# A hybrid encoder layer on one core: the tokens normalised and transposed in two halves, with the V projection between them

## The chip, the core and the metric

The kernel runs on one core of a Trainium2 chip. The metric is the device time of one execution in microseconds, as the median of several executions. The core has four compute engines, which follow their own instruction streams and wait for each other by semaphores: TensorE (PE in the rows; PEld is its loading of weights), VectorE (DVE), ScalarE (ACT) and GpSimd (POOL). SyncE (SP) issues nearly all DMA transfers. Each engine works through its own stream in order, so an instruction that waits holds up everything behind it on its engine.

## The reference

One layer for 512 tokens of width 1024, all float32. The part that the change touches first:

```python
h = rmsnorm(x, pre_mix_norm[l])
proj = h @ w_in[l]
z, xbc, dt_raw, q, k, v, gates = split_cols(proj, IN_SPLITS)
y_ssd = ssd_branch(z, xbc, dt_raw, ...)       # a bidirectional state-space scan, 32 heads
y_attn = window_attention(q, k, v, ...) @ w_attn_out[l]
mixed = (g_ssd * y_ssd + g_attn * y_attn) @ w_o[l]
x = x + rmsnorm(mixed, post_mix_norm[l])
h = rmsnorm(x, pre_mlp_norm[l])
f = jnp.square(jax.nn.relu(h @ w_mlp_in[l])) @ w_mlp_out[l]
x = x + rmsnorm(f, post_mlp_norm[l])
```

## The kernel before

Every product of float32 operands is made of three matmuls on rounded parts: each operand is split into a high part `hi` and a remainder `lo`, and `hi*hi`, `hi*lo` and `lo*hi` are summed in PSUM (`mm3`). So each chunk of weights (128 x 1024 values, 512 KB) is loaded to a raw tile `wr`, ScalarE casts it to `wh`, and GpSimd or VectorE subtracts to get `wl`, in four pieces. Three buffers each hold raw chunks, `wh` and `wl`.

The work is a list of quanta. A quantum is mostly one projection block of 128 output columns for all 512 tokens: 8 steps of k by 3 matmuls, 24 matmuls of 512 columns into one bank of PSUM. `cm` makes such blocks. `tm` makes the V projection with the tokens on the output's partitions: two quanta of two token tiles each (`pair(0)` and `pair(1)`), each 48 matmuls of 256 columns, tile by tile, over two chunks of weights. `dt` (64 columns) is 16 matmuls of 512 columns. The list begins with the two K blocks, then V, dt, and two query blocks.

Before the first quantum, `start` loads the eight tiles of x (four token tiles `t`, two halves `j` of the width, 256 KB each), the identity `ident` for transposes and the gain vector `g`. ScalarE and VectorE square a tile each and sum it, GpSimd makes the reciprocal root `rst`, VectorE scales the tile, and TensorE transposes it in eight 128 x 128 pieces into eight banks of PSUM, one for each k. When all four token tiles are there, ScalarE and VectorE make `h`, hi and lo, from each bank (512 columns at once). Meanwhile `WARM` matmuls on a zero tile keep TensorE busy.

The eight banks of PSUM form two rings: three are called `pp` (blocks of projections), five `ps` (everything else). A tile of a ring waits until the tile that held its bank before has been read for the last time.

The order of the instructions on every engine is not the order of the code. The class `Planner` takes all recorded instructions, with a cost for each, and simulates the five streams; the order that it finds is then forced. So a change of its numbers, or of the code, can move instructions anywhere.

In the MLP, `up_halves` makes the first three blocks for the first 256 tokens before the second 256 have been normalised, and finishes them afterwards; `up_done` then takes relu squared, in place in the bank, and `combine` reads two such banks until its line 1358. At the very end, `down_done` adds the last bank to `acc`, ScalarE squares it for the norm, VectorE multiplies it by the gain `g4`, GpSimd takes the reciprocal root, VectorE scales and adds, and SyncE stores.

Some small constants are broadcast to all partitions by DMA at the start: `dtb` (two rows of 64, for `dt_bias` and `a_log`), `sink` (16) and `dsk` (32, the skip gains, copied by VectorE into `dcol`).

Of the kernel before, what the change touches and what calls it, by code (L numbers as in the profile page):

```python
# [10 lines left out]
F32 = mybir.dt.float32  # L11
F32R = mybir.dt.float32r
AF = mybir.ActivationFunctionType
# [6 lines left out]
NT = 4  # L20
# [10 lines left out]
WARM = 10  # L31
# [44 lines left out]
class Planner:  # L76
# [120 lines left out]
    def duration(self, n):  # L197
# [16 lines left out]
        columns = sum(1 for a in ins if size(a) == 1 and w > 1)  # L214
        if e == "ACT":
            c = (170 if psum else 205) + 0.82 * w + (175 if len(outs) > 1 else 0)
            return c + (85 if columns else 0) * (w < 512 or columns > 1), False
# [10 lines left out]
    def deadlines(self):  # L228

        at, t = {}, 0.0  # L230
        for n, e in enumerate(self.eng):
            if e == "PE":
                at[n] = t
                t += self.cost[n][0]
        late = [0.0] * len(self.ins)
        for n in reversed(range(len(self.ins))):
            e, c = self.eng[n], self.cost[n][0]
            if e == "PE":
                late[n] = at[n]
                continue  # L240
            c += 4000 if e == "SP" else 0
            late[n] = min([late[s] - self.AFTER[self.eng[s]] for s in self.post[n]] + [t + 5000.0]) - c
        return late

    def plan(self, wait=0.3):
# [12 lines left out]
        for _ in self.ins:  # L258
# [20 lines left out]
            if e == "SP":  # L279
                aps = self.operands(self.ins[n].outs)  # L280
                size = 4 * math.prod(d[1] for d in aps[0].ap)
                queue = max(queue, t + 900) + size / 230
# [5 lines left out]
            else:  # L288
# [4 lines left out]
                free[e] = end - self.OVERLAP[e]  # L293
            for s in self.post[n]:
# [22 lines left out]
class Trunk:  # L317
# [196 lines left out]
    def tm(self, c, done):  # L514
# [5 lines left out]
        def pair(t2):  # L520
            ps = self.bank("pp")
# [16 lines left out]
    def start(self):  # L538
        nc = self.nc
        get, put = self.slots.get, self.slots.put  # L540
        self.ident = self.const("ident", [128, 128])
        g = get("g", (128, 128))
        xt = []
        for t in range(NT):
            xt.append([get("x") for _ in range(2)])
            for j in range(2):
                nc.sync.dma_start(xt[t][j], self.d_x[0, t * 128:(t + 1) * 128, j * 512:(j + 1) * 512])
            if t == 0:
                nc.sync.dma_start(self.ident, self.d_cst[:, :128])
                nc.sync.dma_start(g[:8], self.d_pre_mix_norm[0].rearrange("(k p) -> k p", p=128))  # L550
        self.prefetch(2, 0)
# [4 lines left out]
        nc.sync.dma_start(cst, self.d_cst[:, 128:])  # L556
        self.mhalf = self.const("mhalf", [128, 1])
        nc.vector.memset(self.mhalf, -0.5)


        ssq = self.const("ssq0", [128, 8])
        rst = self.const("rst0", [128, 4])
        gT = self.const("gT", [128, 8])
        zero = get("zero", (128, 128))
        nc.vector.memset(zero, 0.0)
        pg = self.bank("ps")
        for _ in range(WARM):
            self.mm(pg[:, :128], zero, zero, True, True)
        put(zero)
        pg = self.bank("ps")  # L570
        self.tr(pg[:, :8], g[:8, :])
        nc.vector.tensor_copy(gT, pg[:, :8])
        put(g)
        ps = [self.bank(tag) for tag in ["pp"] * 3 + ["ps"] * 5]
        for t in range(NT):
            junk = [get("junk") for _ in range(2)]
            nc.scalar.activation(junk[0], xt[t][0], AF.Square, scale=D ** -0.5, accum_out=ssq[:, 2 * t:2 * t + 1])
            nc.vector.tensor_tensor_reduce(junk[1], xt[t][1], xt[t][1], 1.0 / D, EPS, ALU.mult, ALU.add, ssq[:, 2 * t + 1:2 * t + 2])
            put(*junk)
            r = rst[:, t:t + 1]  # L580
            nc.gpsimd.tensor_tensor(r, ssq[:, 2 * t:2 * t + 1], ssq[:, 2 * t + 1:2 * t + 2], op=ALU.add)
            nc.gpsimd.tensor_tensor(r, r, self.mhalf, op=ALU.pow)
            for j in range(2):
                nc.vector.tensor_scalar(xt[t][j], xt[t][j], r, None, op0=ALU.mult)
            for k in range(8):
                self.tr(ps[k][:, t * 128:(t + 1) * 128], xt[t][k // 4][:, (k % 4) * 128:(k % 4 + 1) * 128])
            put(*xt[t])
        self.h = []
        self.prefetch(2, 1)
        for k in range(8):  # L590
            hi, lo = get("h", dtype=F32R), get("h", dtype=F32R)
            self.split_by(hi, lo, ps[k], gT[:, k:k + 1])
            self.h.append((hi, lo))
        self.show("hT", self.h[3][0].bitcast(F32))
# [161 lines left out]
    def kv_quanta(self):  # L756
# [22 lines left out]
        return [self.cm(self.d_w_in, C_K + 128 * i, hh, k_done, ("pppp", "vvpp")[i]) for i in range(2)] + self.tm(C_V, v_done)  # L779
# [594 lines left out]
    def up_halves(self, n):  # L1374
# [148 lines left out]
    def down_done(self, j, t, ps, col):  # L1523
# [17 lines left out]
        nc.vector.tensor_tensor(a, a, self.g4[j][:, col], op=ALU.mult)  # L1541
        if j == 1 and col.stop == 512:
            r = rs[:, n % 2:n % 2 + 1]
            nc.gpsimd.tensor_tensor(r, r, self.mhalf, op=ALU.pow)  # L1544
            for i in range(2):
                x1 = self.x1[t][i]
                for c in [slice(0, 512)] if t < 3 or i == 0 else [slice(0, 256), slice(256, 512)]:
                    nc.vector.scalar_tensor_tensor(x1[:, c], self.acc[t, i][:, c], r, x1[:, c], op0=ALU.mult, op1=ALU.add)  # L1548
# [3 lines left out]
    def build(self):  # L1552
# [3 lines left out]
        self.pair, self.held = [], {}  # L1556
# [4 lines left out]
        self.add(*self.kv_quanta())  # L1561
        self.add(self.dt_quantum())
# [70 lines left out]
```

## Time and profile before

| | |
|---|---|
| median of 3 runs | 1102.45 us (1101.1 to 1104.1) |
| the profiled execution | 1101.8 us, of which its span is 1099.7 us |
| TensorE busy | 1084.1 us, 99% of the span |
| VectorE, ScalarE, GpSimd busy | 711.8, 622.2, 771.5 us |
| DMA | 128 MB, 116 GB/s over the span |

The span is what the profile covers, from the first instruction to the last; 2.1 us of the profiled execution lie outside it. A busy TensorE can still be one that runs at half its clock, so the clock column of the stretches is read beside it.

### The profile page before, as it was taken

To read this page: it belongs to the slowest core of one execution; us is meant where nothing else is said; L and a number is where in the kernel's file an instruction comes from. 1 tells how busy PE (TensorE), PEld (TensorE's weight loads), DVE (VectorE), ACT (ScalarE), POOL (GpSimd) and SP (SyncE) were. 2 spreads that over 40 slices of the span, in tenths; PEclk is the share of its full clock that TensorE was granted. 3 is DMA by queue.
4 is the path that set the end of the run, shared out by engine and by line. 5 is a ranking of instruction groups with operands and counts; after the bars stand their busy time and mean duration, and the time that the engine had idled before them with its cause. 6 is when DMAs were issued, how large, how long until landed. Compare 5 with 4: busy or idle time off the path is not lost.

```text
span 1099.7 us, 16603 instructions
## 1 busy us (share of the span) xinstructions
PE 1084.1 (99%) x5651; PEld 910.7 (83%) x5651; DVE 711.8 (65%) x1229; ACT 622.2 (57%) x1325; POOL 771.5 (70%) x946
## 2 busy tenths in 40 slices
PE   8999999999999999999999999999999999999997
PEld 6988888888888888888888788889788888888886
DVE  6287787687687687788877852425555566564135
ACT  5356776687667767676778532324555444444331
POOL 4436666557668798899989966511679898898842
PEclk8999999999999999999999999999999999999999
DMA  6434433534444536364655563603312522523232
GB/s 191 138 94 118 125 97 100 149 89 115 108 119 140 134 102 174 87 157 122 155 133 149 151 176 114 191 21 115 96 39 77 173 58 81 169 58 98 65 107 76
DMA packets 207584, 128.09 MB, mean 116 GB/s; under 512 B 10851, under 2 KB 192595, under 8 KB 207500
## 3 DMA queue, kind: packets, MB, share of 16 engines
q1 hardware_dynamic: 207500, 127.04, 40.9%
q8 instruction: 44, 0.72, 0.3%
q14 instruction: 40, 0.33, 0.1%
HBM read 124.59 MB, written 2.42 MB: 116 GB/s over the span
## 4 chain that ended last, share of the span: by engine, by line
PE 61%; POOL 1%; DVE 1%; ACT 1%; issue 1%; POOLq 0%; DVEq 0%
PE pp L375 45%; PE ps L375 16%; PE ps L379 1%; POOL wl L454 0%; POOL w L1104 0%; DVE x L1548 0%; POOL frs L1544 0%; POOL w L1103 0%; ACT junk L1534 0%; DVE acc L1532 0%; ACT m L1068 0%; DVE m L1069 0%; POOL ssq L1111 0%; ACT wh L450 0%; DVE yT L1142 0%
## 5 line engine op out<-in xcount | busy, mean ns | idle before, releaser
L454 POOL TENSOR_TENSOR wl<-wr,wh 128x256 fp32r<-128x256 f32 (+1 forms) x513 | 439.6, 885 | 185.6 <-ACT wh L450 180.1
L375 PE MATMUL pp<-h,wh 128*128 128x512 f32 (+1 forms) x1760 | 534.8, 386 | 2.6 <-DVE ft L1356 2.1
L375 PEld LDWEIGHTS pp<-h,wh 128*128 128x128 f32 x1760 | 324.5, 188 | 66.6 <-ACT wh L450 2.3
L375 PE MATMUL pp<-h,wl 128*128 128x512 f32 (+1 forms) x872 | 336.3, 386 | 0.0
L450 ACT CAST wh<-wr 128x1024 fp32r<-128x1024 f32 (+1 forms) x141 | 146.8, 1043 | 172.5 <-PE pp L375 123.7
L375 PEld LDWEIGHTS pp<-h,wl 128*128 128x128 f32 x872 | 163.9, 188 | 32.0
L1452 POOL TENSOR_TENSOR wl<-wd,wh 128x256 fp32r<-128x256 f32 x144 | 117.0, 848 | 13.4 <-ACT wh L1449 11.9
L375 PE MATMUL ps<-wh,fl 128*128 128x512 f32 (+1 forms) x192 | 73.0, 380 | 0.0
L375 PE MATMUL ps<-wh,fh 128*128 128x512 f32 (+1 forms) x192 | 73.0, 380 | 0.0
L375 PE MATMUL ps<-wl,fh 128*128 128x512 f32 (+1 forms) x192 | 73.0, 380 | 0.0
L1067 ACT ACTIVATE n<-cb,tables 128x128 f32<-128x128 f32 x128 | 49.1, 391 | 19.7 <-DVE cb L1058 19.5
L1449 ACT CAST wh<-wd 128x512 fp32r<-128x512 f32 x72 | 41.5, 618 | 31.3 <-PE ps L375 19.8
L899 DVE SCALAR_TENSOR_TENSOR u<-pp,cv,u 128x510 f32<-128x510 f32 (+1 forms) x64 | 47.7, 745 | 5.7 <-ACT u L895 4.3
L1068 ACT ACTIVATE m<-cb,tables 128x128 f32<-128x128 f32 x128 | 48.9, 388 | 3.0 <-DVE cb L1058 3.0
L375 PE MATMUL pp<-yh,wl 128*128 128x512 f32 x128 | 49.9, 390 | 0.3 <-POOL wl L454 0.3
L375 PE MATMUL pp<-yl,wh 128*128 128x512 f32 x128 | 49.8, 389 | 0.0
L375 PE MATMUL pp<-yh,wh 128*128 128x512 f32 x128 | 49.7, 389 | 0.0
L1063 ACT ACTIVATE rf<-rf,tables 128x128 f32<-128x128 f32 x128 | 42.3, 393 | 12.1 <-DMA rf<-csT 12.0
L831 ACT ACTIVATE P<-P,mx 128x384 f32<-128x384 f32 (+1 forms) x64 | 35.2, 553 | 20.5 <-DVE mx L828 20.2
L1061 POOL TENSOR_TENSOR rb<-rb,tables 128x512 f32<-128x512 f32 x32 | 35.7, 1119 | 12.8 <-DMA rb<-csT 5.1
L1103 POOL TENSOR_TENSOR w<-w,E 128x256 f32<-128x256 f32 x48 | 38.4, 812 | 6.3 <-DVE w L1099 4.8
L1320 DVE SCALAR_TENSOR_TENSOR pp<-pp,r 128x256 f32<-128x256 f32 (+1 forms) x24 | 13.5, 563 | 44.7 <-ACT r L1316 44.5
(244 smaller groups left out, 2053.4 us busy)
## 6 DMA issues: line engine op xcount, KB each, us to landing
wr<-in_w_in SPq DMA_DIRECT2D x76, 512.0 KB, 3.9
wr<-in_w_mlp_in SPq DMA_DIRECT2D x32, 512.0 KB, 4.0
wd<-in_w_mlp_out SPq DMA_DIRECT2D x48, 256.0 KB, 4.7
rf<-csT SPq DMA_DIRECT2D x32, 256.0 KB, 4.2
rb<-csT SPq DMA_DIRECT2D x32, 256.0 KB, 5.0
wr<-in_w_ssd_out SPq DMA_DIRECT2D x14, 512.0 KB, 4.6
E<-csE SPq DMA_DIRECT2D x96, 64.0 KB, 3.9
x<-in_x SPq DMA_DIRECT2D x16, 256.0 KB, 3.8
```

The source lines that it names most:

```text
L375: self.nc.tensor.matmul(out, lhsT, rhs, start=start, stop=stop, skip_group_check=more)
L450: self.nc.scalar.copy(hi[:, :m], raw)
L454: engines[e].tensor_tensor(lo[:, c], raw[:, c], hi[:, c].bitcast(F32), op=ALU.subtract)
L831: nc.scalar.activation(p[:, :w], p[:, :w], AF.Exp, bias=mx[:, n:n + 1], accum_out=sm[:, n:n + 1])
L899: nc.vector.scalar_tensor_tensor(u[:, a:e], ps[:, a + d:e + d], self.wtap(t, b), u[:, a:e], op0=ALU.mult, op1=ALU.add)
L1061: nc.gpsimd.tensor_tensor(v4(rb), v4(rb), cs[:, 1].unsqueeze(2).to_broadcast([128, 4, 128]), op=ALU.subtract)
L1063: nc.scalar.activation(v4(rf)[:, h], v4(rf)[:, h], AF.Identity, bias=ncs[:, 0, h:h + 1])
L1067: nc.scalar.activation(v4(n)[:, h], cb[:, 0], AF.Copy, scale=dt[:, 0, h:h + 1])
L1068: nc.scalar.activation(v4(m)[:, h], cb[:, 1], AF.Copy, scale=dt[:, 1, h:h + 1])
L1103: nc.gpsimd.tensor_tensor(wc, wc, E[:, d], op=ALU.add)
L1449: nc.scalar.copy(hi[:, cols], src)
L1452: (nc.vector if q == 512 else nc.gpsimd).tensor_tensor(lo[:, c], src[:, e * q:(e + 1) * q], hi[:, c].bitcast(F32), op=ALU.subtract)
```

## The change

Four edits of the program, and the planner's numbers for DMAs.

1. `start` is split. `start_half(0)` loads, normalises and transposes token tiles 0 and 1 before the first quantum, into four banks (two k to a bank) instead of eight; `start_half(1)` does tiles 2 and 3 and is recorded at quantum 1. `h` is made in pieces of 256 columns. V's two quanta now come first, then dt, then K. Tile j = 0 is scaled by ScalarE, no longer by VectorE. V's first pair uses a bank of the ring `ps`.
2. The identity and the gain vector are issued on ScalarE's queue ahead of its table load; `WARM` goes from 10 to 20, and 8 more matmuls on a scaled tile follow the transposes of token tile 0. The table of constants `cst` is recorded after the first half.
3. `up_halves` takes its third bank from `ps`.
4. In the tail the product with the gain goes to a new tile `ag` instead of back into `acc`.

```diff
-WARM = 10
+WARM = 20
...
+        if e == "ACT" and "DMA" in kind:
+            return 400, False
...
-            c += 4000 if e == "SP" else 0
+            c += 4000 if "DMA" in type(self.ins[n]).__name__ else 0
...
-                queue = max(queue, t + 900) + size / 230
+                queue = max(queue, t + 900) + size / 300
...
+                end += 2500 if "DMA" in type(self.ins[n]).__name__ else 0
...
-            ps = self.bank("pp")
+            ps = self.bank("pp" if t2 else "ps")
...
         self.ident = self.const("ident", [128, 128])
+        nc.scalar.dma_start(self.ident, self.d_cst[:, :128])
         g = get("g", (128, 128))
+        nc.scalar.dma_start(g[:8], self.d_pre_mix_norm[0].rearrange("(k p) -> k p", p=128))
...
+        self.h = [(get("h", dtype=F32R), get("h", dtype=F32R)) for _ in range(8)]
+        self.start_half(0)
+        self.prefetch(2, 1)
+        self.at(1, lambda: self.start_half(1))
+        self.at(1, self.later_constants)
+
+    def start_half(self, t2):
+
+        nc = self.nc
+        get, put = self.slots.get, self.slots.put
+        xt = {}
+        for t in (2 * t2, 2 * t2 + 1):
+            xt[t] = [get("x") for _ in range(2)]
             for j in range(2):
                 nc.sync.dma_start(xt[t][j], self.d_x[0, t * 128:(t + 1) * 128, j * 512:(j + 1) * 512])
+        ps = [self.bank(tag) for tag in (["ps"] * 4 if t2 else ["pp"] * 3 + ["ps"])]
+        for t in xt:
+            junk = [get("junk") for _ in range(2)]
+            ssq, r = self.ssq0[:, 2 * t:2 * t + 2], self.rst0[:, t:t + 1]
+            nc.scalar.activation(junk[0], xt[t][0], AF.Square, scale=D ** -0.5, accum_out=ssq[:, 0:1])
+            nc.vector.tensor_tensor_reduce(junk[1], xt[t][1], xt[t][1], 1.0 / D, EPS, ALU.mult, ALU.add, ssq[:, 1:2])
+            put(*junk)
+            nc.gpsimd.tensor_tensor(r, ssq[:, 0:1], ssq[:, 1:2], op=ALU.add)
+            nc.gpsimd.tensor_tensor(r, r, self.mhalf, op=ALU.pow)
+            nc.scalar.activation(xt[t][0], xt[t][0], AF.Copy, scale=r)
+            nc.vector.tensor_scalar(xt[t][1], xt[t][1], r, None, op0=ALU.mult)
+            for k in range(8):
+                self.tr(ps[k % 4][:, k // 4 * 256 + t % 2 * 128:k // 4 * 256 + t % 2 * 128 + 128],
+                        xt[t][k // 4][:, (k % 4) * 128:(k % 4 + 1) * 128])
             if t == 0:
+                for _ in range(8):
+                    self.mm(self.dummy[:, :128], xt[t][1][:, :128], xt[t][1][:, :128], True, True)
+            put(*xt[t])
+        tok = slice(t2 * 256, t2 * 256 + 256)
+        for k in range(8):
+            hi, lo = self.h[k]
+            self.split_by(hi[:, tok], lo[:, tok], ps[k % 4][:, k // 4 * 256:k // 4 * 256 + 256], self.gT[:, k:k + 1])
...
-        return [self.cm(self.d_w_in, C_K + 128 * i, hh, k_done, ("pppp", "vvpp")[i]) for i in range(2)] + self.tm(C_V, v_done)
+        return self.tm(C_V, v_done) + [self.cm(self.d_w_in, C_K + 128 * i, hh, k_done) for i in range(2)]
...
-                banks.append(self.bank("pp"))
+                banks.append(self.bank("pp" if m < 2 else "ps"))
...
-        nc.vector.tensor_tensor(a, a, self.g4[j][:, col], op=ALU.mult)
+        if col.start == 0:
+            self.ag[t, j] = self.slots.get("ag")
+        nc.vector.tensor_tensor(self.ag[t, j][:, col], a, self.g4[j][:, col], op=ALU.mult)
...
-        self.add(*self.kv_quanta())
-        self.add(self.dt_quantum())
+        kv = self.kv_quanta()
+        self.add(*kv[:2], self.dt_quantum(), *kv[2:])
```

Three places show how instructions move. The first is SyncE's stream from the dt bias to the skip gains, with the DMA semaphore that each issue waits for (a DMA waits for the last DMA that used its semaphore). Before:

```order
L634 DMA v_49_467<-in_pre_mlp_norm 8x128 [waits DMAHW4_49]
L556 DMA cst<-in_cst 128x448 [waits DMAHW5_49]
L360 DMA dtb<-in_dt_bias 128x64 [waits DMAHW6_49]
L360 DMA sink<-in_attn_sink 128x16 [waits DMAHW7_49]
L360 DMA dtb<-in_a_log 128x64 [waits DMAHW0_49]
L360 DMA dsk_550<-in_d_skip 128x32 [waits DMAHW1_49]
```

Now, where `wr_199` is the weights of dt (256 KB) and the last one on semaphore 6 ahead of `dtb`:

```order
L433 DMA wr_199<-in_w_in 128x8x64 [waits DMAHW6_49]
L641 DMA v_45_482<-in_conv_w 112x128 [waits DMAHW7_49]
L642 DMA v_46_483<-in_conv_w 48x128 [waits DMAHW0_49]
L643 DMA v_46_483<-in_conv_b 32x128 [waits DMAHW1_49]
L644 DMA v_46_483<-in_b_gate 16x128 [waits DMAHW2_49]
L645 DMA v_46_483<-in_ssd_norm 16x128 [waits DMAHW3_49]
L646 DMA v_46_483<-in_pre_mlp_norm 8x128 [waits DMAHW4_49]
L606 DMA cst<-in_cst 128x448 [waits DMAHW5_49]
L363 DMA dtb<-in_dt_bias 128x64 [waits DMAHW6_49]
L363 DMA dtb<-in_a_log 128x64 [waits DMAHW7_49]
L363 DMA sink<-in_attn_sink 128x16 [waits DMAHW0_49]
L363 DMA dsk_622<-in_d_skip 128x32 [waits DMAHW1_49]
```

`a_log` has moved ahead of `sink`; `dsk` is still the last of the four. Before, the transfer on semaphore 6 ahead of `dtb` was a V chunk of 512 KB (`wr_227`, of line 430); now it is dt's chunk of 256 KB.

The second place is VectorE's stream at the start. Before, the copies of `dsk` into `dcol` stand behind all of h:

```order
L401 SCALAR_TENSOR_TENSOR h_220<-ps_122,gT,h_219 128x512
L401 SCALAR_TENSOR_TENSOR h_224<-ps_123,gT,h_223 128x512
L454 TENSOR_TENSOR wl_232<-wr_91,wh_231 128x256 x2
L612 COPY dcol<-dsk_550 64x16 x2
L767 TENSOR_TENSOR KL_271<-pp_245,KH_270 64x512
```

Now (x_277 to x_282 are token tiles 2 and 3, ps_285 the first of their banks):

```order
L404 SCALAR_TENSOR_TENSOR h_119<-ps_131,gT,h_118 128x256
L583 ISA junk_290,ssq_75<-x_278 128x512
L583 ISA ssq_75 128x1
L583 ISA junk_306,ssq_75<-x_282 128x512
L583 ISA ssq_75 128x1
L671 COPY rows_271<-ps_269 16x512
L624 COPY dcol<-dsk_622 64x16 x2
L588 TENSOR_SCALAR x_278<-x_278,rst_76 128x512
L588 TENSOR_SCALAR x_282<-x_282,rst_76 128x512
L404 SCALAR_TENSOR_TENSOR h_105<-ps_285,gT,h_104 128x256
```

The copies now stand between the squares of the second half's tiles and their scaling. On ScalarE likewise the exponential of `a_log` (line 729, before 717) now stands ahead of the scaling of the second half's other two tiles.

The third place is TensorE where the first three blocks of the MLP end and the fourth begins. Before:

```order
L375 MATMUL pp_8332<-h_901_8174,wh_7946 128x256
L375 MATMUL pp_8332<-h_902_8175,wh_7946 128x256
L375 MATMUL pp_8332<-h_901_8174,wl_7947 128x256
L375 MATMUL pp_8526<-h_887_8160,wh_8423 128x512
L375 MATMUL pp_8526<-h_888_8161,wh_8423 128x512
```

Now:

```order
L378 MATMUL ps_8366<-h_901_8208,wh_7980 128x256
L378 MATMUL ps_8366<-h_902_8209,wh_7980 128x256
L378 MATMUL ps_8366<-h_901_8208,wl_7981 128x256
L378 MATMUL pp_8560<-h_887_8194,wh_8457 128x512
L378 MATMUL pp_8560<-h_888_8195,wh_8457 128x512
```

The order is the same; the third block's bank is now of the other ring, so that the fourth block (pp_8560) takes the third `pp` bank, last used in the mix, instead of the first block's.

## Rows read from the trace of the kernel before

**Rows 1.** Waits of TensorE, whole span: us in total, times, longest.

```profile
PE pp L379 <- DMA ident<-in_cst: 3.4, 1, 3.4
PE pp L375 <- DVE ft L1356: 2.1, 1, 2.1
PE ps L375 <- ACT pT L848: 0.8, 1, 0.8
```

**Rows 2.** Timeline, start: us, us long, engine, line, tiles, count, idle before.

```profile
1.03 4.24 PE L375 MATMUL ps<-zero 128*128 128x128 f32 x20 [1.03 <-DVE zero L565]
8.61 0.49 DVE L584 TENSOR_SCALAR x<-x,rst 128x512 f32<-128x512 f32 x1 [1.00 <-POOL rst L582]
8.64 0.45 PE L379 MATMUL pp<-ident,x 128*128 128x128 f32 x1 [3.37 <-DMA ident<-in_cst]
10.02 0.16 DVE L572 COPY gT<-ps 128x8 f32<-128x8 f32 x1
11.75 1.05 ACT L450 CAST wh<-wr 128x1024 fp32r<-128x1024 f32 x1 [1.80 <-DMA wr<-in_w_in]
16.33 0.73 PE L375 MATMUL pp<-h,wh 128*128 128x512 f32 x2 [0.52 <-DVE h L401]
```

**Rows 3.** Stretches: us, PE, PEld, DVE, ACT, POOL busy, clock, DMA share, GB/s.

```profile
8.00:15.00 7.00, 6.36 (x29) 5.84 (x29) 4.77 (x11) 2.42 (x6) 3.87 (x8) 0.51 1.09 307
16.33:43.60 27.27, 27.27 (x163) 23.64 (x164) 13.51 (x20) 15.34 (x26) 12.08 (x17) 1.00 0.44 122
```

**Rows 4.** Timeline of SyncE's queue, 15 to 18 us.

```profile
15.79 0.35 SPq L360 DMA_DIRECT2D dtb<-in_dt_bias  x1
16.66 0.44 SPq L360 DMA_DIRECT2D dtb<-in_a_log  x1
17.15 0.43 SPq L360 DMA_DIRECT2D dsk<-in_d_skip  x1
```

**Rows 5.** Timeline: readers of the last constants, and GpSimd beside them.

```profile
20.55 7.36 POOL L454 TENSOR_TENSOR wl<-wr,wh 128x256 fp32r<-128x256 f32 x10 [4.17 <-ACT wh L450]
21.97 0.26 ACT L717 ACTIVATE dtb<-dtb 128x64 f32<-128x64 f32 x1 [0.55 <-DMA dtb<-in_a_log]
22.36 1.38 DVE L612 COPY dcol<-dsk 64x16 f32<-64x16 f32 x2
```

**Rows 6.** Timeline, TensorE in the first query projection.

```profile
44.31 0.39 PE L375 MATMUL pp<-h,wl 128*128 128x512 f32 x1
```

**Rows 7.** GpSimd's splits up to 45 us: busy us, mean ns, idle before.

```profile
L454 POOL TENSOR_TENSOR wl<-wr,wh 128x256 fp32r<-128x256 f32 x21 | 15.4, 770 | 13.6 <-ACT wh L450 13.6
```

**Rows 8.** Timeline, a flip of half the tokens before the MLP.

```profile
742.68 1.91 PE L379 MATMUL ps<-ident,h 128*128 128x128 f32 x16
743.46 2.29 ACT L400 ACTIVATE h<-ps,cv 128x256 fp32r<-128x256 f32 x6
746.09 2.04 DVE L401 SCALAR_TENSOR_TENSOR h<-ps,cv,h 128x256 fp32r<-128x256 f32 x5
```

**Rows 9.** Chain that ended last, 764 to 810 us: start, us, what.

```profile
765.87 6.36 PE pp L375 x52
776.24 0.34 DVE ft L1356
776.72 1.40 PE pp L375 x5
804.21 5.44 PE ps L375 x24
```

**Rows 10.** Timeline there, TensorE and GpSimd.

```profile
774.33 0.28 PE L375 MATMUL pp<-h,wl 128*128 128x256 f32 x1
771.46 10.09 POOL L454 TENSOR_TENSOR wl<-wr,wh 128x256 fp32r<-128x256 f32 x12 [9.48 <-ACT wh L450]
```

**Rows 11.** GpSimd in the tail, and line 370: ns min/median/max.

```profile
1094.26 0.66 POOL L1544 TENSOR_TENSOR frs<-frs,mhalf 128x1 f32<-128x1 f32 x1 [3.00 <-DVE frs L1539]
L370 POOL TENSOR_TENSOR rs<-rs,mhalf x8: 537/543/553, 722.4 to 761.4; 128x1 f32<-128x1 f32 x8
```

More of the change, by code (lines that the diff above doesn't have):

```diff
@@ L541, in start @@
         self.ident = self.const("ident", [128, 128])
+        nc.scalar.dma_start(self.ident, self.d_cst[:, :128])
         g = get("g", (128, 128))
-        xt = []
-        for t in range(NT):
-            xt.append([get("x") for _ in range(2)])
+        nc.scalar.dma_start(g[:8], self.d_pre_mix_norm[0].rearrange("(k p) -> k p", p=128))
+        self.mhalf = self.const("mhalf", [128, 1])
+        nc.vector.memset(self.mhalf, -0.5)
+        self.ssq0 = self.const("ssq0", [128, 8])
+        self.rst0 = self.const("rst0", [128, 4])
@@ new lines, in start @@
+        self.gT = self.const("gT", [128, 8])
+        zero = get("zero", (128, 128))
+        nc.vector.memset(zero, 0.0)
+        self.dummy = self.bank("ps")
+        for _ in range(WARM):
+            self.mm(self.dummy[:, :128], zero, zero, True, True)
+        put(zero)
+        pg = self.bank("ps")
+        self.tr(pg[:, :8], g[:8, :])
+        nc.vector.tensor_copy(self.gT, pg[:, :8])
+        put(g)
+        self.h = [(get("h", dtype=F32R), get("h", dtype=F32R)) for _ in range(8)]
+        self.start_half(0)
@@ L546, in start @@
+        self.prefetch(2, 1)
[7 more added lines that the diff above has]
+            xt[t] = [get("x") for _ in range(2)]
             for j in range(2):
                 nc.sync.dma_start(xt[t][j], self.d_x[0, t * 128:(t + 1) * 128, j * 512:(j + 1) * 512])
-            if t == 0:
-                nc.sync.dma_start(self.ident, self.d_cst[:, :128])
-                nc.sync.dma_start(g[:8], self.d_pre_mix_norm[0].rearrange("(k p) -> k p", p=128))
@@ L551, in start @@
-        self.prefetch(2, 0)
+        ps = [self.bank(tag) for tag in (["ps"] * 4 if t2 else ["pp"] * 3 + ["ps"])]
[12 more added lines that the diff above has]
+                        xt[t][k // 4][:, (k % 4) * 128:(k % 4 + 1) * 128])
+            if t == 0:
+                for _ in range(8):
+                    self.mm(self.dummy[:, :128], xt[t][1][:, :128], xt[t][1][:, :128], True, True)
+            put(*xt[t])
@@ L552, in start, with later_constants @@
+        tok = slice(t2 * 256, t2 * 256 + 256)
+        for k in range(8):
+            hi, lo = self.h[k]
+            self.split_by(hi[:, tok], lo[:, tok], ps[k % 4][:, k // 4 * 256:k // 4 * 256 + 256], self.gT[:, k:k + 1])
+    def later_constants(self):
         cst = self.const("cst", [128, 448])
@@ L555, in start @@
         self.UL = cst[:, :256].rearrange("p (d s) -> p d s", d=2)
[L556 to L594, printed above, removed]
+        self.nc.sync.dma_start(cst, self.d_cst[:, 128:])
     def transpose_split(self, src, name, tag="ps"):
@@ L1547, in down_done @@
                 for c in [slice(0, 512)] if t < 3 or i == 0 else [slice(0, 256), slice(256, 512)]:
-                    nc.vector.scalar_tensor_tensor(x1[:, c], self.acc[t, i][:, c], r, x1[:, c], op0=ALU.mult, op1=ALU.add)
+                    nc.vector.scalar_tensor_tensor(x1[:, c], self.ag[t, i][:, c], r, x1[:, c], op0=ALU.mult, op1=ALU.add)
                     nc.sync.dma_start(self.out[0, t * 128:(t + 1) * 128, i * 512 + c.start:i * 512 + c.stop], x1[:, c])
@@ L1555, in build @@
         self.h2t, self.h2, self.f, self.acc = [], [], {}, {}
-        self.pair, self.held = [], {}
+        self.pair, self.held, self.ag = [], {}, {}
         n = lambda: len(self.quanta)
```

## Prediction

> **What bounds the kernel now.** I read TensorE's waits first, because the page has TensorE busy for 99% of the span. In the whole span three waits stand out: 3.4 us for the identity, 2.1 us for a bank that VectorE has to read (line 1356), 0.8 us for the scores' softmax [rows 1]. So no edit can bring more than it does in one of three places: ahead of TensorE's first gapless stretch, at that bank, or behind its last matmul. Second I read the start's timeline: ten matmuls on the zero tile, 4.24 us long (20 records, two to a float32 matmul, so 0.42 us each), an idle wait of 3.37 us, transposes from 8.64, the first projection at 16.33 [rows 2]. Third the stretches: from 16.33 to 43.60 TensorE is busy 27.27 of 27.27 us at full clock, while from 8 to 15 us the clock is 0.51 and DMA moves 307 GB/s [rows 3]. So the measure for the start is when the two K blocks, V and dt are all done, that is, when the first query block begins. Its third matmul begins at 44.31; two matmuls of 0.2267 us earlier (24 in 5.44 us [rows 9]) is 43.86 [rows 6].
>
> **The start, part by part.** *Weights.* Four x tiles instead of eight lie ahead of the weights, 1 MB less. At 307 GB/s that is 3.4 us, so the first cast goes from 11.75 [rows 2] to about 8.35 and ends 1.05 later, at 9.4. GpSimd then makes eight pieces of `wl` at 0.77 us [rows 7], 6.2 us, to 15.6. The first token tile needs both V chunks, all eight pieces. It ends some three matmuls behind the last of them; the second tile is 24 matmuls of 256 columns at 0.122 us (52 in 6.36 us [rows 9]), 2.9 us. V's first quantum is done at about 18.9.
>
> *The second half.* It can't follow at once. In VectorE's new order the two copies of `dsk` stand ahead of the scaling of tiles 2 and 3, and on ScalarE the exponential of `a_log` does. So the scaling waits for the last of the small broadcasts. Before, `dtb`, `a_log` and `dsk` were issued at 15.79, 16.66 and 17.15 [rows 4]; the reader of `a_log` began at 21.97, waiting for its DMA, and the copies of `dsk` at 22.36 [rows 5]: `dsk` landed between, and I take 22.15. The transfer whose semaphore `dtb` waits for is now 256 KB instead of 512 KB, 0.85 us less at 307 GB/s, so `dsk` lands at about 21.3 (bounds 21.3 and 22.15, if the issue is not earlier). The copies took 1.38 us for two, 0.69 each, beside GpSimd's splits from 20.55 to 27.9 [rows 5]; the nearest copy with GpSimd not splitting, of 8 columns, took 0.16 [rows 2]. Now GpSimd has no chunk to split then. I take 0.16 each, with 0.69 as the other bound: 21.65. Two scalings of 0.49 [rows 2] end at 22.65, transposes of the last tile close the first bank 0.2 later, ScalarE's first piece of h takes 0.38 and VectorE's eight take 0.41 each [rows 8]: 0.2 + 0.38 + 3.3 gives 26.55. The last bank's three matmuls end about 0.35 later, at 26.9; V's other matmuls have gone in between.
>
> The rule that decides between the two prices of the copy is in the Trainium skill, "SBUF — State Buffer", section "Who interferes with whom": VectorE and GpSimd share one pair of ports, a copy can take it, and who comes second is blocked for a whole instruction of the other. By it the 0.69 holds a wait for GpSimd, and without splits the copy is short; by the row alone the same copies cost 0.69 again, and the sum would be 1.06 us more.
>
> *Behind it* 24 matmuls of V at 0.122 (2.9), 14 of dt at 0.2267 (3.2; two of the 16 are earlier) and 48 of K (10.9) follow without a gap, 17.0 us in all: the first query block begins at 43.9, where it was 43.86. **The start gives nothing**: TensorE begins its projections some four microseconds earlier, and idles from about 18.9 to 22.1 instead.
>
> *Free edits.* Ten more warming matmuls are 4.2 us at the row's rate and end between 7.2 and 9.5 (the bounds: all faster once the clock rises, or none). Their cover is TensorE's 3.37 us wait for the identity [rows 2], which the earlier issue on ScalarE takes away. If they end at 9.5 with the eight dummies behind, the first half is about 1.4 us later, V's first quantum later by up to 2.1 with it (21.0), still ahead of 22.1. So they cost nothing while the second half is what is late. The two issues on ScalarE (0.35 to 0.44 each by SyncE's [rows 4]) lie ahead of the first x tile.
>
> **The MLP.** The third half block's last matmul begins at 774.33 [rows 10], 0.122 us long, and the next block begins at 776.72, behind the first block's relu squared and its combination on VectorE, which starts at 776.24 [rows 9]. The weights are not the cause, since GpSimd splits from 771.46 on [rows 10]. In the new order the fourth block takes the third `pp` bank, last used in the mix and long free. The removed wait is 776.72 - 774.33 - 0.12 = **2.27 us**. The next stall would be the fifth block's bank, the first block's: it comes free where the fourth began before, at about 776.7, and is wanted only after the fourth block's work, which began at 774.45 and lasts 5.4 us (24 x 0.2267), at 779.9. So nothing is late next. The bounds are 0, if another wait stands there, and 2.27.
>
> **The tail.** In place, VectorE's product with the gain had to wait until ScalarE had squared the tile, and so ran beside the last reciprocal root; into a new tile it can run ahead. That root took 0.66 us where eight others took 0.543 in the middle [rows 11]. I take 0.12 us off, bounds 0 and 0.12.
>
> **Everything else** (h in pieces of 256 columns, the planner's numbers) I set to 0. TensorE's order behind K is the same, and its remaining wait there is 0.8 us [rows 1]: that is the most to gain, and as much again may be lost.
>
> **Sum:** 0 - 2.27 - 0.12 = about -2.4 us. Against its own time, 1101.8 becomes 1099.4; the median of the runs shown is 0.65 above that profiled execution, so 1102.45 becomes **1100.1**.
>
> **Rivals.**
> *The second half isn't held up.* If the constants land earlier or the order leaves slack, GpSimd's sums and roots for tiles 2 and 3 come behind its splits (15.6) with four small instructions, at about 17.1; scaling ends at 18.1, TensorE is free at 18.9, the first bank closes at 20.5, and the same 0.38 + 3.3 + 0.35 gives 24.5 instead of 26.9. The start then gains 2.3 us: 1097.8. Against it: the issue rows and the order of VectorE, which put `dsk` near 21.3.
> *The clock falls in the new idle time (the slower side).* The stretch from 8 to 15 us ran at 0.51, the lower level of 1.2 GHz, behind an idle wait of 3.37 us [rows 2, 3]. The new wait from 18.9 to 22.1 is 3.2 us long and comes behind a stretch in which TensorE follows GpSimd's pieces and is busy about half. If the clock is low when the second half begins, the 16 transposes, V and dt's first matmuls take twice as long: some 6.8 us of work at half rate, so that the chain ends near 29.5 instead of 26.9, 2.6 us later: 1102.9. It is slower than before from 2.4 us of such loss on; if the low clock lasts through twice as much work, it is 1106.5. For it: those rows. Against it: the ten warming matmuls went at the low rate already, so that no row shows a fall. The Trainium skill, "TensorE: Matmul & The Clock Gate", Part 1, says that the slow clock is the default and activity releases it; by that rule this rival's 1102.9 is what the pause makes.
> *The constants land no earlier and the copies stay long.* 0.85 + 1.06 = 1.9 us on the start: 1102.0.
> *The bank brings nothing,* because something else, such as the five-bank ring that now has one tile more, holds the fourth block for as long: 1102.4.
>
> **How the numbers follow.** Chances: the forecast 0.42 (its own range, with the 0.8 on either side and the bounds of the small terms, 1098.8 to 1101.6); the second half unhindered 0.20; the clock 0.22, of which 0.05 for the long form; late constants 0.09; the bank without effect 0.07. The range 1097.6 to 1104.0 leaves out the long form, the lowest part of the second, and the rest of the edges. A measurement of this kernel can tell about 0.3% from no change, 3.3 us: faster is below 1099.14, slower above 1105.76. Faster has 0.18 of the unhindered case and 0.10 of the forecast's own low edge, 0.28; slower the long form and a little of the clock's edge, 0.06; the same holds 0.66.
>
> **What would show it.** TensorE's wait for the identity is gone and its first V matmul stands near 9.5 to 12; then an idle stretch near 19 to 22, put down to VectorE's scaled tile, with the `dcol` copies right before it behind `dsk`'s DMA, at 0.16 or 0.69; the clock column of the stretch from 22 to 30 tells the second rival; the first query matmul at 43.9; no gap behind the MLP's third half block; the last root near 0.54. The prediction is wrong if the constants come much earlier, if TensorE runs at half clock past 25 us, or if a wait of over 1 us appears between 44 and 770.

## The result, and the profile after

The changed kernel takes 1108.47 us (median of 6 runs, 1105.71 to 1109.49) against 1102.53 for the kernel before, a ratio of 1.0047 with a 95% interval of 1.0031 to 1.0063: slower by about 6 us, outside the range given. The profiled execution has a span of 1107.4 us against 1099.7. These two executions lie 0.7 us above and 0.7 us below the medians of their kernels, so their difference of 7.7 us is larger than that of the medians.

TensorE's waits in the whole span (us in total, times, longest) answer to [rows 1]. The wait for the identity and the one for the MLP's bank are gone, and in their place stand new ones, at the start (x, KL) and in the middle (B and u, inputs of the scan, at line 918):

```profile
PE ps L382 <- DVE B L918: 2.0, 2, 1.8
PE pp L378 <- DVE KL L781: 1.7, 1, 1.7
PE ps L382 <- DVE x L588: 1.4, 1, 1.4
PE ps L382 <- ACT x L587: 1.3, 1, 1.3
PE ps L382 <- DVE u L918: 1.3, 1, 1.3
```

To see where the 7.7 us lie, I matched each of TensorE's matmuls with the one of the kernel before that has as many columns of matmul still behind it, and took the difference of the two start times. What is left of the work is the same, so a difference that grows over a stretch was lost there. The experiments below are in the same table (us; the columns are places, in us, on the time axis of the kernel before; worked out from the start times in the traces). Each row is one execution, the profiled one, and can lie some us off the median of its kernel:

```
                                   81   242   523   725   806
after                            +3.3  +3.3  +9.6 +10.1  +7.9
1  before + bank                  0.0   0.0  -0.5  -0.5  -2.8
2  before + numbers              +0.2  +0.1  +4.5  +4.7  +6.2
3  after with 230                +5.2  +4.8  +5.2  +5.2  +3.0
4  before, middle as after       -0.5  -0.6  +3.7  +3.4  +5.0
5  after, middle as before       +2.9  +2.6  +2.8  +2.8  +0.5
6  after, rstd 2 us later        +1.7  +1.3  +3.4  +3.8  +1.5
7  after with 230, broadcasts    +3.9  +3.5  +3.0  +2.9  +0.7
8  as 7, K ahead of dt           +3.3  +3.3  +2.6  +2.6  +0.3
9  as 5, broadcasts              +1.3  +1.0  +1.5  +1.5  -0.8
10 as 9, K ahead of dt           -0.5  -0.5  -0.3  -0.4  -2.6
11 before + bank + tail          -0.2  -0.2  -0.4  -0.5  -2.7
```

The changed kernel loses 3.3 us up to 81 us, 6.8 from there to 725, and gets 2.2 back at the MLP's bank.

**The start.** The timeline (us, us long, engine, line, tiles, count, idle before) of the place where the second half (token tiles 2 and 3) is due, beside [rows 2, 5]:

```profile
12.12 0.39 PE L378 MATMUL ps<-wh,h 128*128 128x256 f32 x1 [0.24 <-ACT h L403]
...
19.42 0.28 PE L378 MATMUL ps<-wh,h 128*128 128x256 f32 x1
20.07 0.26 ACT L729 ACTIVATE dtb<-dtb 128x64 f32<-128x64 f32 x1 [3.20 <-DMA dtb<-in_a_log]
...
20.99 0.55 PE L382 MATMUL ps<-ident,x 128*128 128x128 f32 x3 [1.29 <-ACT x L587]
...
21.98 0.35 DVE L624 COPY dcol<-dsk 64x16 f32<-64x16 f32 x2 [4.62 <-DMA dsk<-in_d_skip]
22.36 0.88 DVE L588 TENSOR_SCALAR x<-x,rst 128x512 f32<-128x512 f32 x2
...
22.90 1.64 PE L382 MATMUL ps<-ident,x 128*128 128x128 f32 x13 [1.37 <-DVE x L588]
24.25 3.04 ACT L403 ACTIVATE h<-ps,gT 128x256 fp32r<-128x256 f32 x8 [2.24 <-PE ps L382]
...
24.76 3.22 DVE L404 SCALAR_TENSOR_TENSOR h<-ps,gT,h 128x256 fp32r<-128x256 f32 x8 [1.52 <-ACT h L403]
```

V's first quantum begins at 12.12, where the first projection began at 16.33, and its last matmul begins at 19.42. Then TensorE waits twice, 1.29 us for a tile scaled by ScalarE and 1.37 for one scaled by VectorE. ScalarE has just waited 3.20 us for a_log's DMA, VectorE 4.62 us for dsk's. The second half of h ends at 24.76 + 3.22 = 27.98. The stretches show TensorE's clock at 1.00 where it was 0.51 from 8 to 15 us, and 2.70 us without work in the second [rows 3]:

```profile
8.00:15.00 7.00, 6.66 (x50) 5.95 (x51) 4.02 (x12) 6.01 (x13) 5.73 (x10) 1.00 0.83 255
16.33:43.60 27.27, 24.57 (x156) 21.76 (x155) 7.55 (x19) 12.89 (x27) 13.37 (x20) 1.00 0.56 149
```

**K and dt.** Behind the first attention scores (line 378, ps<-KL,Q) TensorE waits again, a wait that [rows 1] don't have:

```profile
58.13 0.28 PE L378 MATMUL ps<-KL,Q 128*128 128x256 f32 x1
...
58.37 0.83 DVE L730 SCALAR_TENSOR_TENSOR dtw<-tables,dtb 128x256 f32<-128x256 f32 x1
...
59.24 0.69 DVE L781 TENSOR_TENSOR KL<-pp,KH 64x512 fp32r<-64x512 f32 x1
...
60.08 0.70 PE L378 MATMUL pp<-h,wh 128*128 128x512 f32 x2 [1.67 <-DVE KL L781]
```

The next block needs the bank of the second K block, and VectorE reads it for the last time at 59.24 (line 781), after a piece of dt's chain (line 730).

**The middle.** VectorE's waits show what is late there: the broadcast of the inverse norms of the scan's output (rstd, 256 KB by DMA, from which VectorE makes the normalised output yT). VectorE waits for it 20.5 us in six places, where the kernel before has 6.0 in two (us in total, times, longest). Changed kernel, then before:

```profile
DVE yT L1154 <- DMA rstd<-rrow: 20.5, 6, 6.3
```

```profile
DVE yT L1142 <- DMA rstd<-rrow: 6.0, 2, 5.5
```

What that does to TensorE is to be read from the chain of waits around 445 us (start, us, what), where TensorE loses 1.3 us:

```profile
438.01 4.80 DMA rstd<-rrow
...
442.84 0.04 DVE yT L1154
...
443.29 2.71 DVE yT L1154 x3
446.00 0.67 DVE u L911
...
446.76 0.64 ACT th L917
...
447.42 0.99 DVE u L918
...
448.45 0.87 PE ps L382 x6
```

VectorE stands at yT (line 1154) until rstd has landed, does its four pieces, and only then the last step of u's convolution (line 911), whose tanh (ScalarE, line 917) and product (line 918) TensorE is waiting for. Yet TensorE needs u at once and yT only in the output projection. The longest wait of the middle, 1.8 us for B near 513 us, has rstd in its chain too, but behind it stands another DMA and 8 us of ScalarE's and VectorE's work:

```profile
491.35 5.13 DMA rstd<-rrow
...
500.68 4.84 DMA rf<-csT
```

The waits at line 918 are 3.3 us of the middle's 6.8; for the rest no single cause is shown.

**The bank and the tail** are as foreseen [rows 9 to 11]: in the MLP the fourth block follows the third half block without a gap, and the last reciprocal root takes 0.54 us.

```profile
784.56 0.28 PE L378 MATMUL ps<-h,wl 128*128 128x256 f32 x1
784.68 0.63 PE L378 MATMUL pp<-h,wh 128*128 128x512 f32 x2
```

```profile
1102.07 0.54 POOL L1558 TENSOR_TENSOR frs<-frs,mhalf 128x1 f32<-128x1 f32 x1 [3.32 <-DVE frs L1551]
```

### The profile page after: what moved, and what is told of

Its sections match the earlier page's. It is cut to its first block, busy times and chain, and to the rows that moved or that the text cites. A ratio compares the mean times of both kernels' runs of the same rounds, so it can differ in the third digit from the quotient of the medians.

```text
span 1107.4 us, 16701 instructions
## 1 busy us (share of the span) xinstructions
PE 1088.2 (98%) x5687; PEld 912.3 (82%) x5687; DVE 713.1 (64%) x1231; ACT 625.6 (56%) x1337; POOL 767.9 (69%) x948
## 4 chain that ended last, share of the span: by engine, by line
PE 77%; DMA 7%; DVE 6%; POOL 3%; ACT 3%; issue 2%; SPq 1%; POOLq 0%; DVEq 0%; ACTq 0%
PE pp L378 56%; PE ps L378 19%; PE ps L382 2%; DMA rstd<-rrow 2%; POOL wl L457 2%; DMA rf<-csT 1%; DVE u L911 1%; DMA rrow<-rcol 1%; DVE yT L1154 1%; DMA x<-in_x 1%; DMA rb<-csT 1%; DMA dsk<-in_d_skip 1%; POOL w L1115 0%; POOL xd L1009 0%; DVE m L1082 0%
## 5 line engine op out<-in xcount | busy, mean ns | idle before, releaser
L378 PE MATMUL pp<-h,wh 128*128 128x512 f32 (+1 forms) x1728 | 528.2, 388 | 1.7 <-DVE KL L781 1.7
L378 PEld LDWEIGHTS pp<-h,wh 128*128 128x128 f32 x1728 | 319.5, 188 | 65.4 <-issue 3.2
L378 PE MATMUL pp<-h,wl 128*128 128x512 f32 (+1 forms) x856 | 331.9, 388 | 0.0
L378 PEld LDWEIGHTS pp<-h,wl 128*128 128x128 f32 x856 | 160.8, 188 | 32.2 <-issue 0.2
L1079 ACT ACTIVATE n<-cb,tables 128x128 f32<-128x128 f32 x128 | 49.5, 391 | 21.3 <-DVE cb L1070 19.7
L378 PEld LDWEIGHTS ps<-wl,fh 128*128 128x128 f32 x192 | 36.1, 188 | 7.0
```

The costliest lines, as they stand in the source:

```text
L378: self.nc.tensor.matmul(out, lhsT, rhs, start=start, stop=stop, skip_group_check=more)
L1079: nc.scalar.activation(v4(n)[:, h], cb[:, 0], AF.Copy, scale=dt[:, 0, h:h + 1])
```

## The experiments

**1. The bank alone.**

```diff
-                banks.append(self.bank("pp"))
+                banks.append(self.bank("pp" if m < 2 else "ps"))
```

> The kernel before with one edit: the third half block of the MLP takes its bank from the other ring. The order of GpSimd and SyncE stays that of the kernel before, and TensorE's differs in the MLP alone. Theory A (the bank wait is a wait of its own, and the loss of the change lies in the order of the middle): the 2.27 us wait behind the third half block goes and nothing else moves, so 1102.5 becomes 1100.2. Rival B (the shifted ring of five banks costs as much elsewhere): no change, 1102.5, with new waits on that ring behind the MLP's first blocks.

Measured: 1100.21 us against 1102.77, ratio 0.9972 (0.9963 to 0.9981). Theory A holds; the wait is gone and nothing comes in its place. 2.0 us of the profiled execution's 2.8 fall between 763 and 803 us; another 0.5 fall by 400 us, at a wait for VectorE that differs between the profiles (0.7 us in the kernel before, 0.4 in experiment 11).

**2. The planner's numbers alone, in the kernel before.**

```diff
+        if e == "ACT" and "DMA" in kind:
+            return 400, False
...
-            c += 4000 if e == "SP" else 0
+            c += 4000 if "DMA" in type(self.ins[n]).__name__ else 0
...
-                queue = max(queue, t + 900) + size / 230
+                queue = max(queue, t + 900) + size / 300
```

> The kernel before with the planner's new numbers for DMAs alone (an assumed rate of 300 instead of 230, the 4000 for every DMA's deadline). The program's work, tiles and banks are those of before; only the order moves. Theory A (the middle's loss comes from the order that these numbers make): TensorE gets new waits between 250 and 520 us, about 7 us in all, and the time is about 1108 to 1110. Rival B (the loss comes from the split start, which turns the ring of SBUF slots and the banks, so that tiles wait for other readers): no more than 0.5 us from before, 1102 to 1103.

Measured: 1105.5 us against 1102.77, ratio 1.0026 (1.0013 to 1.0039), with executions from 1102.49 to 1111.19. The rival's "no more than 0.5 us" is out; theory A has the place right (the table grows by 4.4 between 242 and 523 us, and VectorE waits 19.0 us for rstd) and the size too big: 2.7 us by the medians. The table has 6.2, since its execution lies 2.1 above the median; 1.5 of them, between 763 and 803, fall where the granted clock is low (last section).

**3. The changed kernel with 230 put back.**

```diff
-                queue = max(queue, t + 900) + size / 300
+                queue = max(queue, t + 900) + size / 230
```

> The changed kernel with one number put back: the planner's assumed DMA rate is 230 again. The split start, the bank, the tail and the slots are those of the change. Theory A: the middle's new waits (about 7 us) are gone, what is left is the start's loss of 1.4 to 3 us, the bank's 2.25 and the tail's 0.15 us of gain, so 1101.5 to 1103. Rival B: the middle's waits stay, about 1108.

Measured: 1104.05 us, ratio 1.0007 (0.9999 to 1.0016). One number of the planner takes back 4.4 us. The middle is flat in the table (+4.8 to +5.2), as theory A has it, but the start is worse than with 300, +5.2 instead of +3.3, which put the time 1 us above the expected range. Two things differ there: the first half is late, as experiment 7 shows, and the granted clock from 11 to 15 us is 0.57 (last section).

**4. The kernel before, its middle in the changed kernel's order.** A table gives each engine's order from the first scores to the end of the mix; the planner gets it as a constraint and is free elsewhere.

```diff
     def plan(self, wait=0.3):
+        for some in fixed_order().values():
+            for u, n in zip(some, some[1:]):
+                u, n = u + FIXED_FROM, n + FIXED_FROM
+                if u not in self.pre[n] and u not in self.turn[n]:
+                    self.turn[n].add(u)
+                    self.next[u].append(n)
         late = self.deadlines()
```

> The kernel before, with all instructions from the first attention scores to the end of the mix forced on every engine into the relative order that they have in the changed kernel; the start, the planner's numbers, the tiles and the banks are those of before. Theory A (order alone makes the waits): the waits at some 257, 447 and 513 us appear in this kernel too, 5 to 8 us slower, 1107 to 1110. Rival B (slots and banks): 1102 to 1103, without these waits.

Measured: 1107.74 us against 1102.77, ratio 1.0041 (1.0029 to 1.0053). Tiles, banks, SBUF slots and start are those of before, so the order alone costs 5 us here. In the table 4.3 fall between 242 and 523 us, and 1.6 between 725 and 806, where the granted clock is low (last section). VectorE's wait for rstd came with it:

```profile
DVE yT L1311 <- DMA rstd<-rrow: 19.8, 6, 7.2
```

**5. The converse: the changed kernel, its middle in the order of before.** The same edit with the other table.

> The changed kernel (its start, numbers, bank and tail), with all instructions from the first attention scores to the end of the mix forced on every engine into the relative order of the kernel before. Theory A (the middle's loss is order alone): the waits between 250 and 520 us go, VectorE's wait for rstd falls from 20.5 us to below 10, and what is left is the start's loss of some 3.3 us (1.8 of it the wait for KL at 58 us, which lies ahead of the forced part), the bank's gain of 2.25 and the tail's of 0.15: about 1103.4. Rival B (the slots and banks of the split start make the waits): about 1108.

Measured: 1102.37 us against 1102.46, ratio 0.9997 (0.9988 to 1.0006): 6 us below the changed kernel, with the table flat from 81 to 725 us. Experiments 4 and 5 together settle it: the middle's loss is the order, and neither slots nor banks. What stays is the start: VectorE's waits for rstd, then TensorE's.

```profile
DVE yT L1323 <- DMA rstd<-rrow: 5.5, 2, 5.1
```

```profile
PE pp L547 <- DVE KL L950: 1.6, 1, 1.6
PE ps L551 <- DVE x L757: 1.4, 1, 1.4
...
PE ps L551 <- ACT x L756: 1.0, 1, 1.0
```

**6. One price.** The planner takes rstd's broadcast to land 2 us later.

```diff
-                free[e], end = end, queue + 2000
+                slow = aps[0].tensor.name.startswith("rstd")
+                free[e], end = end, queue + (4000 if slow else 2000)
```

> The changed kernel with one price of the planner moved: it takes the broadcast of the inverse norms (rstd, 256 KB) to land 2 us later than by its rule. Theory A, in its narrow form (VectorE is given yT ahead of the B and u that TensorE waits for, because rstd lands in 5.5 us and not in the 3.8 that the rule gives): VectorE's wait for rstd falls from 20.5 to below 8 us, TensorE's waits for B and u at line 918 go, and half or more of the middle's 6.8 us with them: 1102.5 to 1105.5. Rival C (any order of that kind stalls; rstd is only one place of many): still 1107 or more, with the waits at other tiles.

Measured: 1106.21 us, ratio 1.0029 (1.0017 to 1.0041), with executions from 1102.98 to 1110.2; the profiled one is the shortest of them. In it the narrow theory's signs are all there: the wait for rstd is 6.9 us in one place, TensorE's waits at line 918 are gone, and the middle's growth is 2.1 instead of 6.8.

```profile
DVE yT L1155 <- DMA rstd<-rrow: 6.9, 1, 6.9
```

But the median is 0.7 us above the theory's range, so other executions of the same order lose 3 us more, and which tile they wait for no profile shows. By the medians the price brings 2.3 us. In the table 1.6 lie in the start, where dsk's copies began at 20.33 instead of 21.98, which the edit doesn't aim at. So that VectorE's order around rstd is part of the loss is shown by one execution; how large a part is open.

**7. 230, and the small broadcasts priced 6 us later.**

```diff
-                free[e], end = end, queue + 2000
+                late = aps[0].tensor.name.startswith(("dtb", "dsk"))
+                free[e], end = end, queue + (8000 if late else 2000)
```

> The changed kernel with the assumed DMA rate of 230 and with the small broadcasts dtb and dsk priced 6 us later, so that on VectorE the dcol copies and on ScalarE the exponential of a_log stand behind the scaling of the second half. Theory A (the second half waits for dsk and a_log): the scaling begins at some 17.5 instead of 22 us or later, TensorE's wait for the scaled tile goes, and the start is 2 to 4 us earlier than in the run with 230 alone: 1100 to 1102; the wait for KL at 60 us (1.6 us) stays. Rival D (the second half is late for another reason, such as its tiles' DMAs or GpSimd's splits): 1103.5 to 1104.5, as with 230 alone.

Measured: 1103.23 us, ratio 1.0002 (0.9993 to 1.0011): neither. The copies stand behind the scaling, but the scaling begins at 20.84. In experiment 3 they stood behind it already, so the edit had nothing to move there, and this run doesn't test theory A:

```profile
23.16 0.47 DVE L588 TENSOR_SCALAR x<-x,rst 128x512 f32<-128x512 f32 x1
23.56 1.46 DVE L624 COPY dcol<-dsk 64x16 f32<-64x16 f32 x2
```

The two differ by 1.3 us at 81 us in the table; their granted clocks differ from 11 to 15 us (last section). With 230 the first half is late already; here experiment 7:

```profile
7.92 0.17 DVE L562 COPY gT<-ps 128x8 f32<-128x8 f32 x1 [6.81 <-PE ps L383]
8.00 0.68 DVE L584 CUSTOM_DVE_ANT_0 junk<-x 128x512 f32<-128x512 f32 x1
...
9.70 0.49 DVE L589 TENSOR_SCALAR x<-x,rst 128x512 f32<-128x512 f32 x1 [1.00 <-POOL rst L587]
...
10.24 0.71 PE L379 MATMUL ps<-x 128*128 128x128 f32 x4 [2.35 <-DVE x L589]
```

VectorE's copy of the gains (gT) stands first; it waits until TensorE has done its 20 warming matmuls and transposed the gains. The square of the first tile, its scaling and TensorE's transposes follow, and TensorE idles 2.35 us. In the changed kernel that square ran at 4.64. So rival D was the case in this order, and in it the warming matmuls were not free.

**8. The same, K ahead of dt.**

```diff
-        self.add(*kv[:2], self.dt_quantum(), *kv[2:])
+        self.add(*kv, self.dt_quantum())
```

> The same as the run before it, with K ahead of dt again (V, K, dt). Theory A (with dt ahead, VectorE mixes the chain of the softplus with K's four evictions, so that the query block's bank comes free late): the wait for KL at 60 us goes, 1.6 to 1.8 us less than with dt ahead: 1098.5 to 1100.5. Rival E (the wait belongs to the shifted bank ring and not to the order of the blocks): no difference to dt ahead.

Measured: 1101.94 us, ratio 0.9991 (0.9983 to 1.0000), 1.3 below experiment 7, and the wait for KL is gone from the profile. Theory A holds for the mechanism, with a smaller gain; the level is off because the first half is late, as in experiment 7, and the granted clock from 11 to 15 us is 0.57, as in experiment 3.

**9. The order of before in the middle (as 5), and the broadcasts priced later (as 7, but with 300).**

> The changed kernel with the middle forced into the order of the kernel before (as in the run that gave 1102.4), and with the small broadcasts dtb and dsk priced 6 us later, so that the dcol copies and the exponential of a_log stand behind the scaling of the second half. Theory A (the second half waits for these two, and nothing else is late there): TensorE's two waits of 1.0 and 1.4 us at 20 to 23 us go, the scaling begins near 17.5, the last half of h is done near 25 instead of 28, and the time is 2.5 to 3 us below the same kernel without this: 1099.5. Rival D (something else is as late, such as GpSimd's roots or the tiles' transfers): 1102.0 to 1102.5.

Measured: 1099.63 us against 1102.34, ratio 0.9973 (0.9963 to 0.9983), 2.7 below experiment 5. Theory A holds: TensorE's two waits are gone, and the copies of dsk and the exponential, moved together, were what held up the second half. The table shows 1.6 of it at 81 us, but its execution began late: the same 40 records of warming matmuls took 7.29 us in it and 6.12 in that of experiment 5.

**10. The same, K ahead of dt.**

> The same as the run before it, with K ahead of dt again (V, K, dt). Theory A: TensorE's wait of 1.7 us for KL near 58 us goes too: 1097.7, the fastest of all. Rival E (VectorE has the same work in front of the query block either way): the wait moves to another tile, 1099.5.

Measured: 1098.84 us, ratio 0.9961 (0.9947 to 0.9974), the lowest median of all. The wait for KL is gone, 1.8 us in the table at 81 us. The medians of experiments 9 and 10 differ by 0.8 only, within their intervals. The timeline of the warming and of the second half:

```profile
1.03 7.40 PE L548 MATMUL ps<-zero 128*128 128x128 f32 x40 [1.03 <-DVE zero L724]
...
18.42 0.48 DVE L758 TENSOR_SCALAR x<-x,rst 128x512 f32<-128x512 f32 x1
...
20.59 0.28 PE L548 MATMUL ps<-wh,h 128*128 128x256 f32 x1
...
20.71 1.91 PE L552 MATMUL ps<-ident,x 128*128 128x128 f32 x16
...
22.84 3.23 DVE L574 SCALAR_TENSOR_TENSOR h<-ps,gT,h 128x256 fp32r<-128x256 f32 x8 [2.54 <-ACT h L573]
```

TensorE goes from V's first quantum straight into all 16 transposes.

**11. Before, with bank and tail.** The bank of experiment 1 and the tail of the change.

> The kernel before with the bank of the third half block and the tail's new tile, and its own start and order. Theory A: 2.4 us below before, 1100.1, of which the tail is 0.15 us that the time can't tell but the last root's row can (0.54 instead of 0.66 us). It is the mark that the split start must beat: if the two runs before it are slower than this one, the split start brings nothing here.

Measured: 1099.56 us, ratio 0.9967 (0.9955 to 0.9980); the last roots take 0.54 us. Experiment 10 has 0.9961, and the two intervals overlap: with its start mended and the order kept, the split start is not shown to bring anything beyond the bank and the tail.

## Why the prediction was wrong, point by point

- **"Everything else I set to 0" is the step that failed.** It said that TensorE's order behind K is the same, and took its largest remaining wait, 0.8 us, for the most that could be lost. But the planner's new DMA rate reorders the engines through the middle (experiment 3 puts the rate alone back, and the middle is flat), and small idle times in the kernel before bound what can be gained there, not what can be lost. Experiments 4 and 5 put the order's price at 4 us (experiment 4's growth in the table up to 725) to 6 us (the medians with and without it, experiment 5). The prediction's own sign, a wait of over 1 us between 44 and 770, came: KL at 60, u and B in the middle. With a rate of 300 the planner gives 0.9 + 256 KB/300 GB/s + 2 = 3.8 us to a 256 KB broadcast; in the changed kernel rstd landed 4.7 to 6.3 us after its issue (smallest, median, largest of those that the row could tell):

```profile
DMA to landing us min/median/max: 4.7/5.5/6.3
```

  With 230 it gives 4.0, which is too short as well. Why so small a step changes so much is not shown; that it works through the backlog of the queue, which the rate also sets, is only argued.
- **The start at 0** was mis-sized by 1.4 us. Its mechanism was right: idle time after V's first quantum, behind dsk and a_log. But dsk landed just before 21.98, and not at 21.3 (its bounds were 21.3 and 22.15), and the scaling ended at 23.24 instead of 22.65. The 22.15 that it started from was no reading: the copies in [rows 5] have no wait for dsk, so the row shows only that it had landed by 22.36. The term "transposes of the last tile close the first bank 0.2 later" was 1.0, since 13 of the 16 transposes were still to be done at 22.90. So h was done at 27.98 instead of 26.55 (22.65 + 0.2 + 0.38 + 3.3).
- **"Behind it ... follow without a gap"** held as far as it went: from 24.78 to the scores TensorE has no wait. (The first query block is 2.1 us late: 1.4 by h, and the rest mostly by eight small matmuls of dt, 39.82 to 40.63, that the list leaves out.) But the sum stopped there. That VectorE would mix dt's chain with its reads of K's bank, and keep TensorE waiting 1.7 us for it, was not among the rivals; experiment 10 shows that K ahead of dt takes it away.
- **The copy's price** was right: 0.17 us each against 0.69 in [rows 5]. GpSimd had no instruction between 19.47 and the copies' end. This agrees with the Trainium skill, "SBUF — State Buffer", section "Who interferes with whom", by which VectorE and GpSimd contend only for the ports that they share. The row of the same copy beside the splits would have been the wrong one to take.
- **The clock's rival** did not come: the clock is 1.00 in both stretches. TensorE had no wait of over 1 us from 1.03 to 19.42, and its idle time then fell into pieces of 1.3 and 1.4 us. Whether the longer warming or the missing wait for the identity kept the clock up, no run separates; in experiments 3 and 8, with the same warming, it fell behind a wait of 2.4 us (last section). Two slips of the prediction belong here. "No row shows a fall" is wrong, since the kernel before has 1.00 in the stretch ahead of the 0.51 of [rows 3], with TensorE idle for most of it:

```profile
5.00:8.00 3.00, 0.28 (x3) 0.09 (x1) 1.58 (x4) 1.00 (x3) 0.76 (x3) 1.00 0.92 283
```

  And 1100.1 + 2.6 is 1102.7, not 1102.9.
- **The unhindered second half**, a rival with 2.3 us of gain, is what experiments 9 and 10 built; h ended at 22.84 + 3.23 = 26.07 instead of 24.2 (20.5 + 0.38 + 3.3), because V's first quantum itself ran to 20.7 instead of 18.9. The warming alone took 7.40 us in this execution and 6.23 in the changed kernel's, where V's first quantum ended at 19.7. The gain was 0.5 us by the table.
- **The bank** (2.27 us foreseen, 2.2 in the changed kernel's row of the table) and **the tail** (0.54 us foreseen, 0.54) were right.

## What to carry to other kernels

Where a planner orders the instructions, a number of its model is an edit of the whole kernel: compare the full order on every engine, not the places that the edit's purpose names, and look for instructions that wait for a DMA ahead of work that the bound engine needs at once. A price for a DMA should at least not be shorter than the landings in the trace (here 3.8 us against 4.7 to 6.3); that a longer price is then enough isn't shown, since experiment 6 tried one and its executions differ by 7 us. And when a change bundles a gain with a new order, take them apart: here one line of bank choice is worth 2.6 us alone and the bundle loses 6.

## What the runs showed of the hardware that was not expected

A pause of TensorE of some 2 us can be followed by a low clock, and so cost more than itself; the same pause need not be. In experiment 2 TensorE worked 0.97 us of the 3 from 779 to 782, at the same bank wait as before (stretches: us, busy time of the engines, then the clock third from the end):

```profile
779.00:782.00 3.00, 0.97 (x6) 0.71 (x5) 2.49 (x8) 2.78 (x5) 3.00 (x5) 1.00 0.41 105
782.00:785.00 3.00, 3.00 (x10) 2.36 (x9) 2.47 (x4) 0.53 (x2) 3.00 (x4) 0.59 0.68 205
785.00:788.00 3.00, 3.00 (x12) 2.39 (x11) 0.00 (x0) 0.00 (x0) 0.74 (x2) 0.84 0.35 98
```

The clock then fell to 0.59, a stretch partly at the level of 1.2 GHz, and was back at 1.00 by 788; TensorE did 10 and 12 matmuls in 3 us where it did 14 in the kernel before, and the table grows by 1.5 us. In the profile of the kernel before the same wait (0.89 us busy of 3) left the clock at 1.00:

```profile
774.00:777.00 3.00, 0.89 (x7) 0.70 (x6) 2.36 (x7) 2.51 (x6) 3.00 (x5) 1.00 0.11 30
777.00:780.00 3.00, 3.00 (x14) 2.44 (x13) 2.52 (x5) 0.93 (x2) 3.00 (x4) 1.00 0.72 192
```

Experiment 4 shows the fall as well, 0.68 and 0.75. So the wait at the bank costs 2.2 us in one profile and some 3.7 in two others, which may be why experiment 1 gained 2.6 in the median. The start shows the same with another wait: TensorE idles 2.4 us near 9 us in experiments 3, 7 and 8 alike, and behind it the clock is 0.57 in experiments 3 and 8 and 1.00 in experiment 7 (first experiment 3, then 7):

```profile
11.00:15.00 4.00, 4.00 (x24) 4.00 (x23) 0.49 (x1) 1.66 (x2) 2.23 (x4) 0.57 0.75 169
11.00:15.00 4.00, 3.75 (x31) 3.31 (x30) 1.23 (x3) 2.91 (x6) 2.15 (x5) 1.00 0.79 168
```

Behind the waits of 1.3 to 1.8 us in the changed kernel it stayed at 1.00. The Trainium skill, "TensorE: Matmul & The Clock Gate", Part 1, has it that the slow clock is the default and activity releases it; the traces agree in that the clock came back under work, and show that the same pause doesn't always bring it down. What decides it is open.

Experiments 2 and 6 also scatter, by 9 and 7 us between executions, where experiments 3 and 8 do by 2 with about as many. What their longer executions wait for is open, since a profile shows one execution.
